# Two-layer decoder trunk on one core: VectorE's work around the MLP in another order

## The chip, the core and the metric

One core of a Trainium2 chip runs the whole program. The time is device microseconds (us) of one execution, the median of several runs. The engines are called as in the profile: PE is TensorE's matmul (PEld its weight loads), DVE is VectorE, ACT ScalarE, POOL GpSimd and SP the engine that issues the DMAs.

## What is computed

A trunk of two layers over 512 rows of 1024 columns in float32. Layer 0 mixes by a differential and a dilated attention, layer 1 by a sparse one. What the change touches is the rest of a layer, which is the same in both:

```python
h = h + rms(y, g_mix_post[i])
hn = rms(h, g_mlp_pre[i])
y = jnp.square(jax.nn.relu(hn @ w_mlp_in[i])) @ w_mlp_out[i]
h = h + rms(y, g_mlp_post[i])
gate = jax.nn.sigmoid(h @ w_ple_gate[i])
h = h + gate * (p[i] @ w_ple_proj[i])
```

`w_mlp_in` is 1024 x 4096, `w_mlp_out` 4096 x 1024, `w_ple_gate` 1024 x 1024. The result is the whole h after layer 1.

## The kernel before, in words

**Precision.** Every float32 factor is split into a high part (a cast on ACT) and a low part (the difference, on DVE or POOL). A product is three matmuls: high by high, high by low and low by high (`mm3`).

**Weights.** `Stream` (lines 123 to 166) brings all weights in one fixed sequence of units of 128x1024. SP loads a unit into one of four `raw` buffers; ACT casts it into one of four `wh` buffers (L138), and DVE subtracts into `wl` (L142), or POOL does so in two halves where the unit is marked "p". `ws.next()` takes the next unit, `ws.free(n)` gives n back; only then does `pump` issue the copies and splits of the units four places further on. So the place of `ws.free` in the program is the place of those splits in DVE's order.

**Order.** PE runs in the order of the program. Of the other engines each works through a queue that was fixed when the program was built: among the instructions that were reckoned ready, the one that stands earliest in the program goes first, so an instruction can stand in a queue ahead of others that the program has before it. On the chip a queue is worked off strictly in its order.

**First matrix (the z stage).** `layer_tail` ends the mixer's output projection row tile by row tile (four tiles of 128 rows): `post_norm` adds the normed result to h, `pre_transpose` scales it by the gain, PE transposes it, ACT and DVE split it into `hz` (L259, L260), and `pre_stats` takes the sum of squares; the inverse roots are computed on POOL (L220). The matmuls of the first four of 32 weight units are cut in halves of 256 columns, so that they begin before tiles 2 and 3 are there. `z_evac` takes each block out of PSUM (DVE L857 into a tile `t` of two buffers, then a square on ACT, L858). The splits of the units 1 and 3 are on POOL (`Z_ENG`).

**Sums of weights.** The second matrix is multiplied in the manner of Strassen and Winograd (seven products of half size instead of eight). `block_sums` (line 882) makes the sums of the weight blocks for it during the z stage: for each of 16 pairs of units four DMA loads `b`, four DVE subtractions (L891) and four DMA stores into `tsum`. Its tiles share the tags `ah` and `al` of five buffers each with the tiles `hg` and `junk` of the norms, and with the parts of the second matrix. It stands in the loop from unit 4 on, a pair in every second turn, and the last two pairs behind the loop.

**Second matrix (the y stage).** For each of 16 pairs, DVE makes sums of activation blocks (`sm`, L952 to L954; the tile has the tag `t`, which `z_evac` uses too), ACT and DVE split them (`split`, L930, L931), and PE adds the products 5, 7, 1 and 6 up in PSUM. A second pass makes the products 2, 3 and 4. In its last turn the results are put together on DVE (L1014, L1015, L1017), `post_norm` runs for all four row tiles, and then `ws.free(3)` follows (line 1019).

**Gate.** The gate's projection goes over the row tiles 0, 2, 1, 3; a tile is transposed (L253) in the middle of the one before it. It needs the gate's weight units 0 to 3. Unit 0 is split before the second pass ends, since four `wl` buffers are there and the last turn holds three; units 1 to 3 come with that `ws.free(3)`.

Of the kernel before, what the change touches and what calls it, by code (L numbers as in the profile page):

```python
# [18 lines left out]
P = 128  # L19
# [27 lines left out]


FILL_ENG = "vppvvvvpppppp"
Z_ENG = "vpvp" + "v" * (KF - 4)  # L50
G_ENG = "vvvvvvvv"
ENG_B = ("act", "pool", "act")
ENG_C = ("pool", "vec", "act")
# [4 lines left out]
def trunk_kernel(ctx, tc, A, out):  # L58
# [56 lines left out]
    def keep(n):  # L115
        st_at["keep"] += n
        assert st_at["keep"] <= 320
        return st[:, st_at["keep"] - n : st_at["keep"]]
# [194 lines left out]
            hrow[2 * q + 1] = t[:, 1, :]  # L313


    def post_norm(mp, r, ps2, gpost, ssy):
        yg = mp.tile([P, D], F32, tag="yg", bufs=2, name="yg")
        for n in range(2):
            junk = mp.tile([P, 512], F32, tag="t", bufs=2, name="junk")
            act.activation(junk, ps2[n], AF.Square, scale=1.0 / 32, accum_out=ssy[:, 2 * r + n : 2 * r + n + 1])  # L320
            vec.tensor_tensor(yg[:, n * 512 : (n + 1) * 512], ps2[n], gpost[:, n * 512 : (n + 1) * 512], op=ALU.mult)
        v = stat(1)
        vec.tensor_scalar(v, ssy[:, 2 * r : 2 * r + 1], ssy[:, 2 * r + 1 : 2 * r + 2], EPS, op0=ALU.add, op1=ALU.add)  # L323
        rs = stat(1)
        rsqrt(rs, v, 1)
        for n in range(2):
            hs = hrow[r][:, n * 512 : (n + 1) * 512]
            vec.scalar_tensor_tensor(hs, yg[:, n * 512 : (n + 1) * 512], rs, hs, op0=ALU.mult, op1=ALU.add)  # L328


    def pre_stats(mp, r, rstd):
# [491 lines left out]
    def layer_tail(i, p0, og, oT, hts, last, begin=None):  # L823
        gi = 4 * i
        with tc.tile_pool(name=f"tail{i}", bufs=1) as mp:
# [56 lines left out]
            def block_sums(j):  # L882

                b = [[mp.tile([P, 512], F32, tag=("ah", "al")[q], bufs=5, name="b") for n in range(2)] for q in range(2)]
                c = [slice(0, 512), slice(512, 1024)]
                for q in range(2):
                    for n in range(2):
                        sync.dma_start(b[q][n], A[f"w_mo{i}"][2 * j + q][:, c[n]])
                (b11, b12), (b21, b22) = b
                for d, x, y in ((b11, b12, b11), (b12, b22, b12), (b22, b22, b11), (b21, b22, b21)):  # L890
                    vec.tensor_tensor(d, x, y, op=ALU.subtract)  # L891
                for q in range(2):
                    for n in range(2):
                        sync.dma_start(tsum[i, j, q][:, c[n]], b[q][n])

            for fb in range(NB, KF):
                if fb % 2 == 0:
                    block_sums(fb // 2 - 2)
                h, l = ws.next()
                ps = bank("A", "z")  # L900
                z_part(ps, h, l, 0, 512)
                ws.free()
                z_evac(fb, ps)
            for j in range(KF // 2 - 2, KF // 2):
                block_sums(j)

            pls = [slot(4 + q, f"ple{q}").rearrange("p (r d) -> p r d", d=D) for q in range(2)]
# [25 lines left out]
            def banks(ps):  # L933
                return {p: [bank("AB"[r], f"y{p}{r}") for r in range(2)] for p in ps}
# [13 lines left out]

            for j in range(NP):
                x1, x2 = x[j]  # L950
                sm = mp.tile([P, S], F32, tag="t", bufs=2, name="sm")
                vec.tensor_tensor(sm[:, L], x1[:, R], x2[:, R], op=ALU.add)  # L952
                vec.tensor_tensor(sm[:, R], x1[:, L], x1[:, R], op=ALU.subtract)
                vec.tensor_tensor(x1[:, R], sm[:, L], x1[:, L], op=ALU.subtract)  # L954
                a, a1 = part_tiles(), part_tiles()
                split(a, slice(0, S), sm)
                split(a1, slice(0, S), x1)
                w = ws.next()
                ops = [(5, a, 0, w, 0), (7, a, 1, w, 1)]
                if j < NP - 2:  # L960
                    for r in (1, 0):
                        one(j, r, ops)
                    ws.free()
                w = ws.next()
                ops1 = [(1, a1, 0, w, 0), (6, a1, 1, w, 1)]
                if j < NP - 2:
                    for r in (1, 0):
                        one(j, r, ops1)
                    ws.free()
                else:  # L970
                    held.append((j, ops + ops1))
# [11 lines left out]
            ws.free(4)  # L983

            acc = banks((2, 3, 4))
            for j in range(0, NP, 2):
                ac, a4 = [], part_tiles(j == 0)
                for q in range(2):
                    x1, x2 = x[j + q]
                    vec.tensor_tensor(x1[:, R], x2[:, L], x1[:, R], op=ALU.subtract)  # L990
                    if q == 1:
                        split(a4, R, x1[:, R])
                    else:
                        split(a4, L, x1[:, R])
                    ac.append(part_tiles(j + q == 0))
                    split(ac[q], slice(0, S), x2)
                ops = []
                w0, w4, w1 = ws.next(), ws.next(), ws.next()
                for q, w in ((0, w0), (1, w1)):
                    ops.append([(2, ac[q], 0, w, 0), (3, a4, q, w, 1)])  # L1000
                ops4 = [[(4, ac[q], 1, w4, q)] for q in range(2)]
                if j == NP - 2:
                    new_big()
                    xg = make_xt([0, 1], [2, 3], KD, f"hg{i}")
                    ssy = keep(8)
                    for r in range(2):
                        d11, d12, d21, c22 = dt[r]
                        for q in range(2):
                            one(j + q, r, ops[q])
                        if r == 1:  # L1010
                            pre_transpose(mp, 0, None, xg)
                        for q in range(2):
                            one(j + q, r, ops4[q])
                        vec.tensor_tensor(d11, acc[2][r], d11, op=ALU.add)  # L1014
                        vec.tensor_tensor(d12, acc[3][r], d12, op=ALU.add)  # L1015
                        post_norm(mp, r, (d11, d12), gpost, ssy)
                        vec.tensor_tensor(d21, d21, acc[4][r], op=ALU.subtract)  # L1017
                        post_norm(mp, r + 2, (d21, c22), gpost, ssy)
                    ws.free(3)
                    continue  # L1020
                for r in range(2) if j == 0 else (None,):
                    rs = range(2) if r is None else (r,)
                    for q, o in ((0, ops[0]), (0, ops4[0]), (1, ops4[1]), (1, ops[1])):
                        for rr in rs:
                            one(j + q, rr, o)
                ws.free(3)
# [33 lines left out]
            for r in (2, 1, 3):  # L1060
                next(g0), next(g0)
                pre_transpose(mp, r, None, xg)
                next(g0), next(g0)
            drain(g0)
            drain(proj(xg, 512, [2] * 4, range(NR), gate1, halves=last))
# [336 lines left out]
```

## Time and profile before

| | |
|---|---|
| median of 3 runs | 1348.42 us (1345.66 to 1348.67) |
| the profiled execution | 1345.57 us, of which the span of the trace is 1343.8 us |
| PE busy | 1295.6 us (96% of the span) |
| DVE busy | 961.1 us (72%) |
| ACT busy | 656.5 us (49%) |
| POOL busy | 167.0 us (12%) |
| moved by DMA | 227.73 MB, 169 GB/s over the span |
| mean granted clock of PE | 0.987 of full speed |

The page gives busy time for each engine, a strip of 40 slices, and the chain of work that ended last; of that chain PE has 77%, DVE 13%. PE is nearly always busy, so what can be gained lies where it waits, and where it runs at a lower clock behind a wait. In the trace layer 0's z stage is at 276 to 458 us, its y stage to 617, its gate to about 680; layer 1's begin at 940, 1128 and 1283.

### The profile page before, as it was taken

The numbers are of one execution on the slowest core, as the hardware profiler recorded it, in microseconds if no ns is written. First come the engines' busy times: TensorE is split into PE (matmuls) and PEld (weight loads), VectorE is DVE, ScalarE is ACT, GpSimd is POOL, SyncE is SP. The second block draws the span as 40 slices with busy tenths as digits, with TensorE's granted clock in tenths as the row PEclk, the third lists the DMA queues.
The fourth block names the chain that finished last, engine by engine and source line by source line (L and its number), as shares of the span: only waits on it lengthen the run. The fifth ranks groups of instructions, "written<-read, shape, count | busy, mean of one in ns | idle before, by whom it ended". The sixth has DMA issues, their size and how long they took to land.

```text
span 1343.8 us, 18709 instructions
## 1 busy us (share of the span) xinstructions
PE 1295.6 (96%) x6617; PEld 1088.2 (81%) x6617; DVE 961.1 (72%) x1761; ACT 656.5 (49%) x1229; POOL 167.0 (12%) x161
## 2 busy tenths in 40 slices
PE   9999989999999899997998999999899998999978
PEld 7888878888888788886897679998888887888867
DVE  6678676476555699768568999966755567987674
ACT  4245476343222465564446668844322225656542
POOL 4212101030000000000013844311200000000000
PEclk9999999999999999998999999999999999999989
DMA  8312242369989655563243240011888896566621
GB/s 294 103 63 71 64 126 82 123 215 313 297 302 313 219 190 196 194 192 106 79 151 126 90 123 33 2 63 63 264 295 293 290 321 212 190 199 194 199 82 48
DMA packets 91534, 227.73 MB, mean 169 GB/s; under 512 B 10288, under 2 KB 11440, under 8 KB 91440
## 3 DMA queue, kind: packets, MB, share of 16 engines
q1 hardware_dynamic: 91440, 226.54, 50.8%
q8 instruction: 52, 0.85, 0.3%
q14 instruction: 42, 0.34, 0.1%
HBM read 184.55 MB, written 41.94 MB: 169 GB/s over the span
## 4 chain that ended last, share of the span: by engine, by line
PE 77%; DVE 13%; DMA 4%; issue 2%; ACT 2%; POOL 1%; SPq 1%; DVEq 0%; ACTq 0%; POOLq 0%
PE y L212 22%; PE z L212 21%; PE pj L212 21%; PE pv L212 3%; PE sc L212 3%; DMA b<-in_w_mo_dram 3%; DVE wl L142 2%; DVE work L1233 2%; PE trp L372 2%; DVE m L1232 2%; PE ak L212 1%; DVE b L891 1%; PE tr L253 1%; PE ple L212 1%; DVE h L328 1%
## 5 line engine op out<-in xcount | busy, mean ns | idle before, releaser
L142 DVE TENSOR_TENSOR wl<-raw,wh 128x1024 fp32r<-128x1024 f32 (+2 forms) x242 | 297.8, 1235 | 69.3 <-ACT wh L138 66.3
L138 ACT CAST wh<-raw 128x1024 fp32r<-128x1024 f32 (+3 forms) x254 | 261.8, 1034 | 172.3 <-PE pj L212 45.5
L212 PE MATMUL y<-wh,ah 128*128 128x512 f32 x432 | 169.6, 393 | 6.5 <-ACT ah L930 6.5
L891 DVE TENSOR_TENSOR b<-b 128x512 f32<-128x512 f32 x128 | 88.0, 691 | 121.4 <-DMA b<-in_w_mo_dram 113.0
L212 PE MATMUL y<-wh,al 128*128 128x512 f32 x432 | 169.7, 393 | 0.5 <-DVE al L931 0.5
L212 PE MATMUL y<-wl,ah 128*128 128x512 f32 x432 | 169.3, 392 | 0.0
L212 PE MATMUL pj<-wh,big 128*128 128x512 f32 (+1 forms) x444 | 151.3, 390 | 3.0 <-DVE big L260 3.0
L220 POOL TENSOR_TENSOR st<-st,mhalf 128x1 f32<-128x1 f32 (+1 forms) x41 | 29.9, 728 | 862.6 <-DVE st L323 745.2
L212 PE MATMUL z<-hz1L,wh 128*128 128x512 f32 (+1 forms) x288 | 106.1, 368 | 3.1 <-DVE hz1L L260 3.1
L212 PE MATMUL z<-hz0L,wh 128*128 128x512 f32 (+1 forms) x288 | 106.1, 368 | 2.1 <-DVE hz0L L260 2.1
L212 PE MATMUL z<-hz1H,wl 128*128 128x512 f32 (+1 forms) x288 | 106.1, 368 | 1.0 <-DVE wl L142 1.0
L212 PE MATMUL z<-hz0H,wl 128*128 128x512 f32 (+1 forms) x288 | 106.0, 368 | 0.6 <-DVE wl L142 0.6
L212 PE MATMUL z<-hz1H,wh 128*128 128x512 f32 (+1 forms) x288 | 106.2, 369 | 0.2 <-ACT hz1H L259 0.2
L212 PE MATMUL z<-hz0H,wh 128*128 128x512 f32 (+1 forms) x288 | 106.1, 368 | 0.2 <-ACT hz0H L259 0.2
L212 PEld LDWEIGHTS y<-wh,ah 128*128 128x128 f32 x432 | 81.9, 190 | 24.2 <-ACT ah L930 7.3
L212 PEld LDWEIGHTS pj<-wh,big 128*128 128x128 f32 x444 | 83.6, 190 | 21.3 <-DVE big L260 3.9
L212 PEld LDWEIGHTS y<-wh,al 128*128 128x128 f32 x432 | 81.9, 190 | 18.5 <-DVE al L931 1.3
L212 PEld LDWEIGHTS y<-wl,ah 128*128 128x128 f32 x432 | 81.8, 189 | 16.9
L858 ACT ACTIVATE a<-t 128x512 f32<-128x512 f32 x40 | 25.3, 632 | 125.5 <-DVE t L857 125.5
L212 PEld LDWEIGHTS z<-hz1L,wh 128*128 128x128 f32 x288 | 55.1, 191 | 11.9 <-DVE hz1L L260 3.3
L212 PEld LDWEIGHTS z<-hz0L,wh 128*128 128x128 f32 x288 | 55.0, 191 | 11.0 <-DVE hz0L L260 2.3
L212 PEld LDWEIGHTS z<-hz1H,wl 128*128 128x128 f32 x288 | 55.0, 191 | 10.3 <-DVE wl L142 1.6
(620 smaller groups left out, 2777.4 us busy)
## 6 DMA issues: line engine op xcount, KB each, us to landing
raw<-in_w_mi_dram SPq DMA_DIRECT2D x64, 512.0 KB, 5.1
b<-in_w_mo_dram SPq DMA_DIRECT2D x128, 256.0 KB, 5.3
tsum_dram<-b SPq DMA_DIRECT2D x128, 256.0 KB, 3.4
raw<-tsum_dram SPq DMA_DIRECT2D x32, 512.0 KB, 3.2
raw<-tsum_dram SPq DMA_DIRECT2D x64, 256.0 KB, 3.1
raw<-in_w_mo_dram SPq DMA_DIRECT2D x32, 512.0 KB, 3.7
raw<-in_w_ab_dram SPq DMA_DIRECT2D x20, 512.0 KB, 5.1
raw<-in_w_mo_dram SPq DMA_DIRECT2D x32, 256.0 KB, 2.6
```

The costliest lines, as they stand in the source:

```text
L138: act.copy(h[:, :n], raw[:, :n])
L142: (pool if e == "p" else vec).tensor_tensor(l[:, c], raw[:, c], f32(h[:, c]), op=ALU.subtract)
L212: pe.matmul(ps, a, b, start=first, stop=last, skip_group_check=True)
L220: pool.tensor_tensor(dst, src, mhalf[:, :n], op=ALU.pow)
L253: pe.transpose(ps[:, i * P : (i + 1) * P], src(k), ident)
L328: vec.scalar_tensor_tensor(hs, yg[:, n * 512 : (n + 1) * 512], rs, hs, op0=ALU.mult, op1=ALU.add)
L372: pe.transpose(ps[:, i * P : (i + 1) * P], pt[:, OFF[qt] + kt * P : OFF[qt] + (kt + 1) * P], ident)
L858: act.activation(at[-1][:, fb % 4, :], t, AF.Square)
L891: vec.tensor_tensor(d, x, y, op=ALU.subtract)
L1232: vec.max(m8, w)
L1233: vec.match_replace(w, m8, w, MARK)
```

## The change

`post_norm` takes its second half ready-made if it is given one (`done`), and its square is a function of its own. The splits of the first four units of `w_mlp_in` all go to DVE. `block_sums` begins at unit 6 instead of 4, and three pairs instead of two stand behind the loop. `sm` has a tag of its own with two buffers. In the second pass the square and the gain of the quarter that is already final (`c22`) are taken in turn j = 2. In the last turn, `post_norm` of tile 0 stands ahead of tile 0's product 4; `ws.free(3)` follows the last product; behind it come the norm of tile 2 (`low(0)`), the sums of the other half and the norm of tile 1; the norm of tile 3 (`low(1)`) stands in the gate, after the transposes of tile 2.

```diff
@@ -47,7 +47,8 @@
 
 
 FILL_ENG = "vppvvvvpppppp"
-Z_ENG = "vpvp" + "v" * (KF - 4)
+Z_ENG = "v" * KF
+SUMS = 6
 G_ENG = "vvvvvvvv"
 ENG_B = ("act", "pool", "act")
 ENG_C = ("pool", "vec", "act")
@@ -313,19 +314,24 @@
             hrow[2 * q + 1] = t[:, 1, :]
 
 
-    def post_norm(mp, r, ps2, gpost, ssy):
+
+    def post_norm(mp, r, ps2, gpost, ssy, done=None):
         yg = mp.tile([P, D], F32, tag="yg", bufs=2, name="yg")
-        for n in range(2):
-            junk = mp.tile([P, 512], F32, tag="t", bufs=2, name="junk")
-            act.activation(junk, ps2[n], AF.Square, scale=1.0 / 32, accum_out=ssy[:, 2 * r + n : 2 * r + n + 1])
-            vec.tensor_tensor(yg[:, n * 512 : (n + 1) * 512], ps2[n], gpost[:, n * 512 : (n + 1) * 512], op=ALU.mult)
+        half = [yg[:, :512], yg[:, 512:] if done is None else done]
+        for n in range(len(ps2)):
+            square(mp, r, n, ps2[n], ssy)
+            vec.tensor_tensor(half[n], ps2[n], gpost[:, n * 512 : (n + 1) * 512], op=ALU.mult)
         v = stat(1)
         vec.tensor_scalar(v, ssy[:, 2 * r : 2 * r + 1], ssy[:, 2 * r + 1 : 2 * r + 2], EPS, op0=ALU.add, op1=ALU.add)
         rs = stat(1)
         rsqrt(rs, v, 1)
         for n in range(2):
             hs = hrow[r][:, n * 512 : (n + 1) * 512]
-            vec.scalar_tensor_tensor(hs, yg[:, n * 512 : (n + 1) * 512], rs, hs, op0=ALU.mult, op1=ALU.add)
+            vec.scalar_tensor_tensor(hs, half[n], rs, hs, op0=ALU.mult, op1=ALU.add)
+
+    def square(mp, r, n, src, ssy):
+        junk = mp.tile([P, 512], F32, tag="t", bufs=2, name="junk")
+        act.activation(junk, src, AF.Square, scale=1.0 / 32, accum_out=ssy[:, 2 * r + n : 2 * r + n + 1])
 
 
     def pre_stats(mp, r, rstd):
@@ -894,14 +900,14 @@
                         sync.dma_start(tsum[i, j, q][:, c[n]], b[q][n])
 
             for fb in range(NB, KF):
-                if fb % 2 == 0:
-                    block_sums(fb // 2 - 2)
+                if fb >= SUMS and fb % 2 == 0:
+                    block_sums((fb - SUMS) // 2)
                 h, l = ws.next()
                 ps = bank("A", "z")
                 z_part(ps, h, l, 0, 512)
                 ws.free()
                 z_evac(fb, ps)
-            for j in range(KF // 2 - 2, KF // 2):
+            for j in range((KF - SUMS) // 2, KF // 2):
                 block_sums(j)
 
             pls = [slot(4 + q, f"ple{q}").rearrange("p (r d) -> p r d", d=D) for q in range(2)]
@@ -948,7 +954,7 @@
 
             for j in range(NP):
                 x1, x2 = x[j]
-                sm = mp.tile([P, S], F32, tag="t", bufs=2, name="sm")
+                sm = mp.tile([P, S], F32, tag="sm", bufs=2, name="sm")
                 vec.tensor_tensor(sm[:, L], x1[:, R], x2[:, R], op=ALU.add)
                 vec.tensor_tensor(sm[:, R], x1[:, L], x1[:, R], op=ALU.subtract)
                 vec.tensor_tensor(x1[:, R], sm[:, L], x1[:, L], op=ALU.subtract)
@@ -983,6 +989,20 @@
             ws.free(4)
 
             acc = banks((2, 3, 4))
+            ssy = keep(8)
+
+            def top(r):
+                d11, d12, d21, c22 = dt[r]
+                vec.tensor_tensor(d11, acc[2][r], d11, op=ALU.add)
+                vec.tensor_tensor(d12, acc[3][r], d12, op=ALU.add)
+                post_norm(mp, r, (d11, d12), gpost, ssy)
+
+            def low(r):
+                d11, d12, d21, c22 = dt[r]
+                if r == 0:
+                    vec.tensor_tensor(d21, d21, acc[4][r], op=ALU.subtract)
+                post_norm(mp, r + 2, (d21,), gpost, ssy, c22)
+
             for j in range(0, NP, 2):
                 ac, a4 = [], part_tiles(j == 0)
                 for q in range(2):
@@ -1002,22 +1022,28 @@
                 if j == NP - 2:
                     new_big()
                     xg = make_xt([0, 1], [2, 3], KD, f"hg{i}")
-                    ssy = keep(8)
                     for r in range(2):
                         d11, d12, d21, c22 = dt[r]
                         for q in range(2):
                             one(j + q, r, ops[q])
                         if r == 1:
                             pre_transpose(mp, 0, None, xg)
+                        else:
+                            top(0)
                         for q in range(2):
                             one(j + q, r, ops4[q])
-                        vec.tensor_tensor(d11, acc[2][r], d11, op=ALU.add)
-                        vec.tensor_tensor(d12, acc[3][r], d12, op=ALU.add)
-                        post_norm(mp, r, (d11, d12), gpost, ssy)
-                        vec.tensor_tensor(d21, d21, acc[4][r], op=ALU.subtract)
-                        post_norm(mp, r + 2, (d21, c22), gpost, ssy)
                     ws.free(3)
+                    low(0)
+                    vec.tensor_tensor(dt[1][0], acc[2][1], dt[1][0], op=ALU.add)
+                    vec.tensor_tensor(dt[1][1], acc[3][1], dt[1][1], op=ALU.add)
+                    vec.tensor_tensor(dt[1][2], dt[1][2], acc[4][1], op=ALU.subtract)
+                    post_norm(mp, 1, dt[1][:2], gpost, ssy)
                     continue
+                if j == 2:
+
+                    for r in range(2):
+                        square(mp, 2 + r, 1, dt[r][3], ssy)
+                        vec.tensor_tensor(dt[r][3], dt[r][3], gpost[:, S:], op=ALU.mult)
                 for r in range(2) if j == 0 else (None,):
                     rs = range(2) if r is None else (r,)
                     for q, o in ((0, ops[0]), (0, ops4[0]), (1, ops4[1]), (1, ops[1])):
@@ -1060,6 +1086,8 @@
             for r in (2, 1, 3):
                 next(g0), next(g0)
                 pre_transpose(mp, r, None, xg)
+                if r == 2:
+                    low(1)
                 next(g0), next(g0)
             drain(g0)
             drain(proj(xg, 512, [2] * 4, range(NR), gate1, halves=last))
```

## Rows read from the trace of the kernel before

**Rows 1.** Waits of PE: engine line waited for: us in total, times, longest us.

```profile
PE pj L212 <- DVE wl L142: 11.2, 2, 5.6
PE y L212 <- ACT ah L930: 6.5, 2, 3.2
PE z L212 <- DVE hz1L L260: 3.1, 1, 3.1
PE pj L212 <- DVE big L260: 3.0, 2, 1.5
PE z L212 <- DVE hz0L L260: 2.1, 1, 2.1
...
PE z L212 <- DVE wl L142: 1.6, 3, 0.7
```

**Rows 2.** Windows: from:to, length, busy of PE, PEld, DVE, ACT, POOL, clock, DMA, GB/s.

```profile
293.00:297.00 4.00, 4.00 (x23) 4.00 (x24) 0.34 (x1) 0.00 (x0) 0.00 (x0) 0.62 0.98 313
...
462.00:467.00 5.00, 4.78 (x13) 3.50 (x14) 4.59 (x11) 1.62 (x3) 0.00 (x0) 0.66 0.72 247
467.00:608.00 141.00, 141.00 (x623) 116.72 (x622) 118.61 (x173) 84.19 (x114) 0.00 (x0) 1.00 0.59 190
...
626.00:631.00 5.00, 4.48 (x15) 3.83 (x16) 4.56 (x6) 0.85 (x2) 0.88 (x1) 0.55 0.40 127
```

**Rows 3.** Windows of layer 1, the same columns.

```profile
958.00:962.00 4.00, 3.82 (x19) 3.82 (x20) 1.39 (x3) 0.00 (x0) 0.00 (x0) 0.57 0.90 276
962.00:1107.00 145.00, 145.00 (x680) 121.74 (x680) 83.87 (x111) 41.48 (x52) 0.00 (x0) 1.00 0.89 297
```

**Rows 4.** Timeline of PE at layer 0's gate: start us, us, operation [idle before <-releaser].

```profile
617.34 0.39 PE L212 MATMUL pj<-wh,hg0H 128*128 128x512 f32 x1
...
626.52 0.80 PE L212 MATMUL pj<-wl,hg0H 128*128 128x512 f32 x1 [5.63 <-DVE wl L142]
```

**Rows 5.** Timeline of DVE in the same stretch.

```profile
610.72 0.68 DVE L1014 TENSOR_TENSOR d<-y,d 128x512 f32<-128x512 f32 x1
...
625.25 1.22 DVE L142 TENSOR_TENSOR wl<-raw,wh 128x1024 fp32r<-128x1024 f32 x1
```

**Rows 6.** Groups of DVE, 608 to 631 us: busy us, mean ns of one, idle before.

```profile
L142 DVE TENSOR_TENSOR wl<-raw,wh 128x1024 fp32r<-128x1024 f32 x5 | 6.0, 1221 | 2.4 <-ACT wh L138 2.4
L328 DVE SCALAR_TENSOR_TENSOR h<-yg,st,h 128x512 f32<-128x512 f32 x8 | 5.7, 749 | 0.7 <-POOL st L220 0.4
```

**Rows 7.** Timeline of DVE and POOL at the start of layer 0's MLP.

```profile
274.43 2.33 DVE L142 TENSOR_TENSOR wl<-raw,wh 128x1024 fp32r<-128x1024 f32 x1
...
292.06 1.28 DVE L260 TENSOR_TENSOR hz0L<-tr,hz0H 128x512 fp32r<-128x512 f32 x2
...
274.39 7.46 POOL L142 TENSOR_TENSOR wl<-raw,wh 128x512 fp32r<-128x512 f32 x4 [1.32 <-ACT wh L138]
```

**Rows 8.** Timeline of PE, the same start.

```profile
290.34 0.38 PE L212 MATMUL z<-hz0H,wh 128*128 128x256 f32 x1 [0.24 <-ACT hz0H L259]
292.80 0.58 PE L212 MATMUL z<-hz0L,wh 128*128 128x256 f32 x1 [2.08 <-DVE hz0L L260]
```

**Rows 9.** Chain that ended last, start of layer 1's MLP: start us, us, what.

```profile
946.98 0.45 PE tr L253 x4
...
948.30 6.99 DMA b<-in_w_mo_dram
```

**Rows 10.** Timeline of DVE and PE where layer 0's second matrix begins.

```profile
453.23 0.69 DVE L857 SCALAR_TENSOR_TENSOR t<-z,rb 128x512 f32<-128x512 f32 x1 [3.31 <-PE z L212]
...
459.27 0.41 DVE L952 TENSOR_TENSOR sm<-big 128x256 f32<-128x256 f32 x1
...
461.87 0.50 PE L212 MATMUL y<-wh,ah 128*128 128x512 f32 x1 [3.24 <-ACT ah L930]
```

**Rows 11.** Timeline near the end of the first matrix: DVE of layer 0, PE of layer 1.

```profile
438.31 1.22 DVE L142 TENSOR_TENSOR wl<-raw,wh 128x1024 fp32r<-128x1024 f32 x1
...
1108.59 0.50 PE L212 MATMUL z<-hz1H,wl 128*128 128x512 f32 x1 [0.33 <-DVE wl L142]
```

## The prediction

> **What bounds the kernel now.** I read the waits of PE first, since PE is the engine with nearly all of the time. They show one pattern: PE waits long at three places of the MLP, once per layer each [rows 1], and the releaser is DVE or, behind it, ACT. Then I read the granted clock in windows round those places: behind the long waits PE runs for some microseconds near the lower of its two levels (1.2 of 2.4 GHz; 0.55 to 0.66 as a mean of the window) [rows 2, 3]. So a place costs its waits and the slow stretch behind them, length times (1 - clock). Last I read DVE's timeline to see what stood ahead of the releaser.
>
> **Gate (C).** PE has finished the second matrix and starts the gate at 617.34 [rows 4]. It waits 1.51 us for the split transposes (3.0 for both layers, two waits) and 5.63 us for the split of unit 1 [rows 1, 4]. That split begins at 625.25, although DVE has been at the norms since 610.72 without a pause [rows 5]: six sums and eight gain products of 0.68 each like the first, and eight updates of h of 0.75, lie ahead of it or around it [rows 5, 6]. The slow stretch costs 5 x (1 - 0.55) = 2.3 us [rows 2]. Sum 9.4 us per layer.
>
> **Second matrix (B).** PE waits 3.24 us at 461.87 for the first split activations: DVE begins `sm` only at 459.27 [rows 10], behind the last z block, because both take turns in the two buffers of `t`. The slow stretch costs 5 x (1 - 0.66) = 1.7 us [rows 2], and 0.2 us follows for the low part. Sum 5.1 us; the two waits of [rows 1] are alike (6.5 together, longest 3.2), so 5.1 for layer 1.
>
> **First matrix (A).** In layer 0 PE waits 0.6 us for unit 0's split, 0.24 for ACT and 2.08 for DVE's `hz0L` [rows 1, 8]; that instruction begins at 292.06 [rows 7], behind weight sums that waited for their loads. The slow stretch costs 4 x (1 - 0.62) = 1.5 [rows 2]. Sum 4.4 us. In layer 1 the wait is 3.1 [rows 1] and the slow stretch 4 x (1 - 0.57) = 1.7 [rows 3]: with 0.9 for the small ones, 5.7 us.
>
> All three together: 2 x 9.4 + 2 x 5.1 + 4.4 + 5.7 = 39.1 us, the most that the change can win there. For scale: 0.3% of the time, about what a measurement of this kernel can tell from no change, is 4 us.
>
> **The gate after the change.** Counted by starts, a 512-wide operation of DVE takes 0.6 us, an update of h 0.67, a split 1.14, each some 0.08 under its duration, since the next one begins before it ends [rows 5, 6]. From 610.72 DVE's order becomes: two sums 1.2, two gain products 1.2, a small one 0.15, 0.85 until POOL's root is there (a ready sum of tile 2, 0.6, fits in it), tile 0's h 1.35, split of unit 1 1.14, two transposed halves 1.2, tile 2's one gain product 0.75 with its small one (the other half was done in turn 2), the splits of units 2 and 3 2.3 (covering the next root), tile 2's h 1.35. That is 11.5, so tile 2 is ready at 622.2, its first half at 621.5. PE gets to its transposes 12 matmuls after 617.34; at 141 / 623 = 0.226 us each [rows 2] that is 620.05: a wait of 1.5. Behind it stand, on DVE, the sums of tile 1 (1.8), its gain products (1.35) and then tile 2's transposed half (0.6): 625.95, where PE comes at about 625.8. So 1.7 us remain, if nothing comes between. The high end is 5.5: tile 1's h (1.35) ahead of the transposed half, and a slow stretch of 2.3. I take 2.6, near the low end, since the wait of 1.5 per layer of [rows 1] is of the same size and the slow stretch stands behind the 5.6. Later tiles have 6 us between transposes for some 5 us of DVE: hidden. The two squares and two products of turn 2 lie in a pass in which DVE is busy 118.6 of 141 us [rows 2]: hidden, and if not, under 3 us per layer. Gain 6.8 per layer, 13.6.
>
> **The second matrix after.** With its own buffers `sm` of pairs 0 and 1 needs only the first four blocks, and the parts need `ah` and `al`, free once the last weight sums are stored, over 10 us ahead of the end of z. DVE stands idle before the last z blocks (3.31 us ahead of the last but one [rows 10]), so parts and low parts are there when PE comes; weight units are, as before, four ahead. I leave 0.3 us. Gain 4.8 per layer, 9.6.
>
> **The first matrix after.** POOL's four pieces run from 274.39 for 7.46 us, and DVE's split next to them takes 2.33 instead of 1.22 [rows 6, 7]. On DVE alone four splits are done at 274.43 + 4 x 1.14 = 279.0, where POOL's last ended at 281.85: DVE gets two splits more (2.3) but none of four instructions is lengthened (4.4). The 0.6 for unit 0 goes. SP's queue holds the fifth to eighth weight loads, which wait for these splits, ahead of the loads `b`; those now go out up to 2.8 us earlier, but the second of them needs a buffer that PE's transposes of tile 2 release, 0.6 earlier than before. The chain shows the price: from those transposes to the landing, 948.30 + 6.99 [rows 9], which is slow because the weight loads are still under way. With them gone I estimate 4.5; then the sums are done as the transposes of tile 3 arrive, and ACT's 0.24 and a half low part, 0.6, remain. Bounds: nothing left but these 0.8, or the wait as before (2 to 3, with its slow stretch). I take 1.0. Unit 6 as the first turn I cost at nothing: all sums already run ahead of their place in the program, and two units later (11 us at 5.4) the last would still end before z does. Gain 3.4 and 4.7 so far.
>
> But z has a second limit. DMA share is 0.89 at 297 GB/s over 145 us [rows 3], and splits of units stand on DVE behind sums that wait for `b`. In layer 0 the split of unit 29 is done at 439.45 [rows 11]; PE needs it three units of 24 matmuls (16.3) before 458.6, at 442.3: 2.9 us in hand. In layer 1 PE already waits 0.33 there [rows 11]. With the loads some 2 us earlier (between 0.6 and 2.8), layer 0 keeps its 3.4, layer 1 gets only 2.0 of 4.7. Gain 5.4.
>
> The rows put the limit where the transfers are. The Trainium skill, "SBUF — State Buffer", § A bandwidth-pool intuition that's wrong, gives about 358 GB/s between HBM and a core; by that the 43 MB of [rows 3] would take an estimated 120 us, the stage would have room, and layer 1 would keep 4.7: 1314.2 in all. The rows decide: DVE does wait there.
>
> **Sum.** 13.6 + 9.6 + 5.4 = 28.6 us off the profiled execution's 1345.57: 1317.0. That execution lies 2.85 under the median of the runs (1348.42) and at their lowest (1345.66); I leave the sum as it is.
>
> **Rivals.**
> 1. The z stage gives everything back: if the loads don't move earlier in either layer, PE stands longer near unit 29 and A gains about nothing: 1345.6 - 23.2 = 1322.4. For it: DMA share and the wait of [rows 3, 11]. Against: 2.9 us in hand in layer 0. Chance 0.18. The same section of the Trainium skill has HBM as nearly always the end-to-end bottleneck; that is this rival.
> 2. The z stage has room after all, and the gate goes near its low bound (1.7): A 8.1, B 9.6, C 15.4: 1312.5. For it: less DMA in the way at the start. Against: [rows 11]. Chance 0.14.
> 3. `sm` is early but its parts are not, since `ah` and `al` are held by the last sums: B keeps its waits, 1326.6. Against: the sums end well ahead of z. Chance 0.07.
> 4. The order at the gate comes out as before, because ready instructions may overtake: C stays, 1330.6. Against: the late splits stand behind the norms in the program, and there they are in the trace. Chance 0.04.
> 5. Slower: the parts of the first pairs, now ready early in z, take two of five buffers of `ah` and `al` before the weight sums get them and hold them until y. Then one pair of sums is under way at a time. Counting a load of 7.0 [rows 9], four subtractions of 0.6 and a store, taken at half the load, 12.9 per pair and 206 for 16, against the some 165 that z has: 40 more per layer, 1345.6 + 80 - 23 = 1402. It decides as soon as a part is handed out before the last sum. Against: in the trace `b` waits for the buffers of earlier tiles in the program's order [rows 9]. Chance 0.04.
>
> The forecast has 0.53: 1317, on its own 1312 to 1321.
>
> **Numbers.** Cases 0.53, 0.18, 0.14, 0.07 and 0.04 lie below 1341, so faster has 0.94 after a little is kept for errors of the count; slower 0.04, same 0.02. The range goes from 1307, where all 39.1 are won, to 1328, just over rival 3; only rivals 4 and 5 lie outside.
>
> **What would show it.** Right: PE's wait for `wl` at the gate gone and one of 1 to 2.5 us at the transposes of tile 2; no wait of PE at the first `y` and a clock of 1.00 there; the wait for `hz0L` under 1 us; POOL without splits there; waits of PE for `wl` near the end of layer 1's z. Wrong: a new wait of over 3 us at any of these, or weight sums that end behind z.

## The result, and the profile after

The changed kernel takes 1316.96 us (median of 4 runs, 1314.9 to 1319.21) beside 1348.32 us before (median of 4): a ratio of 0.9772 with a 95% interval of 0.9752 to 0.9792. The predicted 1317.0 is within 0.1 us of that. The parts of the sum are not so close, and the experiments are about them. The profiled execution took 1319.21 us with a span of 1317.4, the longest of the four; line numbers have moved on (the matmuls are L213 now, the weight sums L897).

The waits of PE (engine, line, waited for: us in total, times, longest), with the MLP's entries:

```profile
PE tr L254 <- issue: 3.7, 2, 1.9
...
PE tr L254 <- DVE st L343: 1.7, 2, 0.9
...
PE z L213 <- DVE hz0L L261: 0.3, 1, 0.3
PE z L213 <- DVE hz1L L261: 0.3, 1, 0.3
```

The first four entries of [rows 1] are gone or small. New are two: 1.9 us per layer at the transposes of tile 2 in the gate, and 0.9 per layer at those of tile 2 in z.

For the rest I mark three stages in PE's timeline, the same in all kernels: z from its first matmul to the start of its last, y from there to the gate's first matmul, and the gate from there to the transposes of tile 1.

| us | z, layer 0 | z, layer 1 | y, layer 0 | y, layer 1 | gate, layer 0 | gate, layer 1 |
|---|---|---|---|---|---|---|
| before | 182.47 | 184.21 | 159.10 | 159.01 | 18.69 | 18.45 |
| changed | 179.82 | 179.45 | 153.44 | 153.45 | 13.13 | 13.15 |
| gain | 2.65 | 4.76 | 5.66 | 5.56 | 5.56 | 5.30 |
| predicted | 3.4 | 2.0 | 4.8 | 4.8 | 6.8 | 6.8 |

The gains add up to 29.5 us. Where the code is the same, the profiled execution was longer, by 1.5 us ahead of the first z and by 1.6 between the gate of layer 0 and the z of layer 1, which leaves the 26.4 between the two spans (1343.8 and 1317.4). The medians are 31.4 apart; the predicted sum of 28.6 lies between.

**Gate.** PE's timeline (start, us, operation [idle before <- releaser]):

```profile
610.57 0.39 PE L213 MATMUL pj<-wh,hg0H 128*128 128x512 f32 x1
...
615.52 1.32 PE L254 MATMUL tr<-ident,h 128*128 128x128 f32 x8 [1.89 <-issue]
...
623.70 1.03 PE L254 MATMUL tr<-ident,h 128*128 128x128 f32 x8
```

DVE's timeline next to it:

```profile
603.95 0.68 DVE L996 TENSOR_TENSOR d<-y,d 128x512 f32<-128x512 f32 x1
...
611.53 2.35 DVE L143 TENSOR_TENSOR wl<-raw,wh 128x1024 fp32r<-128x1024 f32 x2
613.80 0.21 DVE L325 TENSOR_SCALAR st<-st 128x1 f32<-128x1 f32 x1
613.92 0.68 DVE L1037 TENSOR_TENSOR d<-y,d 128x512 f32<-128x512 f32 x1
614.67 0.75 DVE L330 SCALAR_TENSOR_TENSOR h<-yg,st,h 128x512 f32<-128x512 f32 x1
615.34 0.74 DVE L330 SCALAR_TENSOR_TENSOR h<-d,st,h 128x512 f32<-128x512 f32 x1
```

The profile puts the 1.89 us down to "issue", that is, to nothing it shows; but PE goes on 0.1 us after DVE has written the first half of tile 2's h (614.67 + 0.75 = 615.42). By starts the chain from 603.95 is done at 616.00, after 12.05 us where I had counted 11.5: the small instruction of tile 2 (`st`) stands behind the splits of units 2 and 3 and not ahead of them, so they no longer cover POOL's root, and a sum of tile 1 stands in between.

Windows of the changed kernel (from:to, length, busy of PE, PEld, DVE, ACT, POOL, clock, DMA, GB/s): the two gates behind that wait, the start of z behind its waits, the two starts of y, and z in both layers.

```profile
616.00:621.00 5.00, 5.00 (x19) 3.92 (x18) 4.94 (x10) 2.40 (x6) 0.55 (x1) 0.66 0.24 92
1268.00:1273.00 5.00, 5.00 (x18) 4.00 (x19) 4.93 (x10) 2.35 (x6) 0.55 (x1) 0.66 0.22 88
...
292.00:297.00 5.00, 4.64 (x37) 4.45 (x38) 2.08 (x4) 1.74 (x3) 0.00 (x0) 1.00 0.70 244
...
457.40:462.40 5.00, 5.00 (x24) 4.15 (x23) 4.31 (x6) 3.60 (x5) 0.00 (x0) 1.00 0.89 271
1109.10:1114.10 5.00, 5.00 (x23) 4.13 (x22) 3.51 (x5) 3.15 (x4) 0.00 (x0) 1.00 1.02 379
...
297.00:437.00 140.00, 140.00 (x650) 117.31 (x649) 85.42 (x117) 41.82 (x55) 0.00 (x0) 1.00 0.89 297
949.00:1089.00 140.00, 140.00 (x651) 117.32 (x650) 86.68 (x118) 42.52 (x55) 0.00 (x0) 1.00 0.89 304
```

At the gates the granted clock is 0.66 as a mean of the 5 us: 5 x (1 - 0.66) = 1.7 us lost per layer, which the prediction had left out of its sum. At y PE runs at full clock and has no wait.

**Start of z.** PE's timeline in layer 0:

```profile
284.52 0.63 PE L254 MATMUL tr<-ident,hg 128*128 128x128 f32 x4 [0.86 <-DVE st L343]
...
292.01 0.38 PE L213 MATMUL z<-hz0H,wh 128*128 128x256 f32 x1 [0.24 <-ACT hz0H L260]
292.74 0.39 PE L213 MATMUL z<-hz0L,wh 128*128 128x256 f32 x1 [0.34 <-DVE hz0L L261]
```

and DVE's:

```profile
275.96 4.63 DVE L143 TENSOR_TENSOR wl<-raw,wh 128x1024 fp32r<-128x1024 f32 x4
...
283.69 0.69 DVE L353 TENSOR_TENSOR hg<-h,gpre 128x512 f32<-128x512 f32 x1
```

Of the waits of [rows 8] ACT's 0.24 stays and DVE's 2.08 is down to 0.34, with the clock at 1.00 behind them (window from 292). In the new order of DVE's queue the second gain product of tile 2 stands behind the four splits in one row and the norm of tile 3. It begins at 283.69, and PE waits 0.86 for it, which I had not seen. (The profile names `st`, the small instruction behind the product, which the transposes do not read.)

### The profile page after: what moved, and what is told of

Its sections match the earlier page's. It is cut to its first block, busy times and chain, and to the rows that moved or that the text cites. A ratio compares the mean times of both kernels' runs of the same rounds, so it can differ in the third digit from the quotient of the medians.

```text
span 1317.4 us, 18700 instructions
## 1 busy us (share of the span) xinstructions
PE 1290.8 (98%) x6617; PEld 1085.0 (82%) x6617; DVE 959.6 (73%) x1765; ACT 655.5 (50%) x1229; POOL 152.2 (12%) x153
## 4 chain that ended last, share of the span: by engine, by line
PE 87%; DVE 8%; ACT 2%; issue 2%; POOL 1%; DMA 1%; SPq 0%; DVEq 0%; ACTq 0%; POOLq 0%
PE z L213 26%; PE y L213 23%; PE pj L213 23%; PE sc L213 4%; PE pv L213 3%; DVE work L1261 2%; PE trp L378 2%; DVE m L1260 2%; PE tr L254 1%; DVE wl L143 1%; PE ak L213 1%; PE ple L213 1%; PE trq L398 1%; PE pva L213 1%; DMA xraw<-in_xT_dram 1%
## 5 line engine op out<-in xcount | busy, mean ns | idle before, releaser
L143 DVE TENSOR_TENSOR wl<-raw,wh 128x1024 fp32r<-128x1024 f32 (+3 forms) x246 | 297.6, 1217 | 67.0 <-ACT wh L139 64.4
L897 DVE TENSOR_TENSOR b<-b 128x512 f32<-128x512 f32 x128 | 87.9, 690 | 115.9 <-DMA b<-in_w_mo_dram 107.4
L213 PE MATMUL y<-wh,ah 128*128 128x512 f32 x432 | 168.3, 390 | 0.0
L213 PE MATMUL y<-wh,al 128*128 128x512 f32 x432 | 168.1, 389 | 0.0
L213 PE MATMUL y<-wl,ah 128*128 128x512 f32 x432 | 168.1, 389 | 0.0
L213 PE MATMUL pj<-wh,big 128*128 128x512 f32 (+1 forms) x444 | 152.5, 394 | 0.0
L213 PE MATMUL z<-hz1H,wh 128*128 128x512 f32 (+1 forms) x288 | 105.6, 367 | 0.2 <-ACT hz1H L260 0.2
L213 PE MATMUL z<-hz0H,wh 128*128 128x512 f32 (+1 forms) x288 | 105.6, 367 | 0.2 <-ACT hz0H L260 0.2
L213 PE MATMUL z<-hz0L,wh 128*128 128x512 f32 (+1 forms) x288 | 105.4, 366 | 0.3 <-DVE hz0L L261 0.3
L213 PE MATMUL z<-hz1L,wh 128*128 128x512 f32 (+1 forms) x288 | 105.4, 366 | 0.3 <-DVE hz1L L261 0.3
L213 PE MATMUL z<-hz0H,wl 128*128 128x512 f32 (+1 forms) x288 | 105.5, 366 | 0.0
L213 PE MATMUL z<-hz1H,wl 128*128 128x512 f32 (+1 forms) x288 | 105.3, 366 | 0.0
L213 PEld LDWEIGHTS pj<-wh,big 128*128 128x128 f32 x444 | 84.5, 192 | 18.7 <-issue 0.7
L213 PEld LDWEIGHTS y<-wh,ah 128*128 128x128 f32 x432 | 81.1, 188 | 16.8
L213 PEld LDWEIGHTS y<-wh,al 128*128 128x128 f32 x432 | 81.1, 188 | 16.7
L213 PEld LDWEIGHTS y<-wl,ah 128*128 128x128 f32 x432 | 81.1, 188 | 16.7
L213 PEld LDWEIGHTS z<-hz0L,wh 128*128 128x128 f32 x288 | 54.3, 189 | 9.3 <-DVE hz0L L261 0.5
L213 PEld LDWEIGHTS z<-hz1L,wh 128*128 128x128 f32 x288 | 54.3, 189 | 9.3 <-DVE hz1L L261 0.5
L213 PEld LDWEIGHTS z<-hz1H,wh 128*128 128x128 f32 x288 | 54.3, 189 | 9.3 <-ACT hz1H L260 0.5
```

The costliest lines, as they stand in the source:

```text
L143: (pool if e == "p" else vec).tensor_tensor(l[:, c], raw[:, c], f32(h[:, c]), op=ALU.subtract)
L213: pe.matmul(ps, a, b, start=first, stop=last, skip_group_check=True)
```

## The experiments

Stages of all runs, as above, in us; the two kernels of the table before are left out.

| kernel | z0 | z1 | y0 | y1 | gate0 | gate1 | median, runs |
|---|---|---|---|---|---|---|---|
| b_zeng | 179.46 | 179.46 | 159.66 | 159.72 | 18.78 | 18.79 | 1340.85, 4 |
| b_sm | 183.37 | 184.01 | 153.44 | 153.44 | 18.28 | 18.42 | 1337.65, 4 |
| b_gate | 182.96 | 183.22 | 159.74 | 159.72 | 11.57 | 11.57 | 1333.20, 4 |
| b_sums | 182.98 | 183.71 | 159.82 | 159.07 | 18.84 | 18.77 | 1348.83, 10 |
| a_vpvp | 186.06 | 183.62 | 153.44 | 153.44 | 11.52 | 13.14 | 1328.02, 4 |
| a_sm_t | 179.46 | 179.46 | 159.66 | 159.75 | 11.52 | 11.52 | 1327.37, 4 |
| a_sums4 | 179.64 | 179.61 | 153.44 | 153.44 | 11.57 | 13.14 | 1318.02, 4 |
| x_more | 185.35 | 185.43 | 153.45 | 153.45 | 11.55 | 11.54 | 1327.84, 1 |
| after2 | 179.52 | 179.46 | 153.45 | 153.44 | 13.15 | 13.16 | 1318.88, 4 |
| v_gate | 179.47 | 179.80 | 153.47 | 153.44 | 10.90 | 10.92 | 1312.20, 4 |
| v_gate2 | 179.48 | 179.48 | 153.44 | 153.44 | 10.93 | 10.92 | 1313.83, 5 |
| v_both | 179.77 | 184.63 | 153.44 | 153.44 | 10.93 | 10.92 | 1315.64, 5 |

### Each part alone, on the kernel before

```diff
b_zeng: -Z_ENG = "vpvp" + "v" * (KF - 4)
        +Z_ENG = "v" * KF
b_sm:   -sm = mp.tile([P, S], F32, tag="t", bufs=2, name="sm")
        +sm = mp.tile([P, S], F32, tag="sm", bufs=2, name="sm")
b_sums: -if fb % 2 == 0: block_sums(fb // 2 - 2)
        +if fb >= 6 and fb % 2 == 0: block_sums((fb - 6) // 2)
b_gate: the diff's hunks from post_norm on, without sm's tag, SUMS = 4
```

> The kernel before with one part of the change: the splits of z units 1 and 3 on DVE. Theory: this alone makes all of z's gain, 2.7 us in layer 0 and 4.8 in layer 1 (the last z block ends that much sooner after the first), some 7 us in all; the wait for wl near unit 29 of layer 1 is gone, and a new wait of about 0.9 us stands at the transposes of tile 2. Rival, the prediction's second limit with SUMS = 6 as what lifted it: layer 1 gains 2 us and keeps waits for wl near unit 29.

> The kernel before with sm in buffers of its own. Theory: y, counted from the last z block to the first matmul of the gate, loses 5.6 us in each layer, 11.2 in all, and PE does not wait at the first y. Rival: part of y's gain comes from the sums moved or the weight units of z; then y loses under 4 us per layer here.

> The kernel before with the last turn of y, the norms and the turn j = 2 of the changed kernel, and nothing else of it. Theory: from the gate's first matmul to the transposes of tile 1 it takes 5.3 to 5.6 us less per layer, some 11 in all, with a wait of about 1.9 us at the transposes of tile 2 and a clock of 0.66 in the 5 us behind it. Rival, the prediction's sum: 6.8 per layer, 13.6 in all.

> The kernel before with the sums of weights begun at unit 6 instead of 4. Theory: nothing changes, within 1.5 us, since DVE's queue has the same order. Rival: the later first pair frees the end of layer 1's z; then its wait for wl near unit 29 goes and the time falls by 2 to 3 us.

Against the kernel before (1348.59 us, 13 runs) the ratios are 0.9938 (0.9917 to 0.9958) for b_zeng, 0.9915 (0.9900 to 0.9930) for b_sm, 0.9884 (0.9865 to 0.9903) for b_gate and 0.9996 (0.9984 to 1.0007) for b_sums: 7.7, 10.9, 15.4 and -0.2 us, 33.8 in all beside the 31.4 of the whole change. b_gate's profiled execution lacks both slow stretches that the changed kernel has at the gate, 3.2 us; that may be the difference.

- b_zeng makes all of z's gain. Layer 1 goes to 179.46 without the sums moved and without `sm`'s buffers, so the rival of a limit that SUMS lifted falls.
- b_sm makes all of y's gain. Its y, without the two squares and products of turn j = 2, is as long as that of the changed kernel which has them (153.44): they are hidden.
- b_sums does nothing, and DVE's queue is in the order of the kernel before. The number in the program is not the place in the queue.
- b_gate gains 7.1 and 6.9 us at the gate, over the 5.6 and 5.3 of the changed kernel: my expectation missed, and the prediction's 6.8 is near. DVE's order there is the same and so is PE's wait; the slow stretch is missing. The parts of this reordering were not tried one by one. b_gate, PE's timeline:

```profile
625.30 1.27 PE L254 MATMUL tr<-ident,h 128*128 128x128 f32 x8 [1.84 <-issue]
...
631.91 1.03 PE L254 MATMUL tr<-ident,h 128*128 128x128 f32 x8
```

and its windows behind the wait in both layers:

```profile
626.00:631.00 5.00, 5.00 (x24) 4.17 (x25) 4.94 (x10) 2.96 (x7) 0.55 (x1) 1.00 0.17 66
1285.00:1290.00 5.00, 5.00 (x25) 4.16 (x24) 4.93 (x10) 2.79 (x7) 0.55 (x1) 1.00 0.21 81
```

b_sm shows the rest of the mechanism at the start of z, where POOL still splits. Its PE timeline in layer 0 and layer 1's window behind the like wait of 4.0:

```profile
295.59 0.39 PE L212 MATMUL z<-hz0L,wh 128*128 128x256 f32 x1 [3.79 <-DVE hz0L L260]
```

```profile
956.90:961.90 5.00, 4.96 (x25) 4.96 (x26) 1.24 (x2) 0.01 (x1) 0.00 (x0) 0.55 0.92 299
```

DVE's timeline of b_sm ahead of it:

```profile
291.45 0.69 DVE L891 TENSOR_TENSOR b<-b 128x512 f32<-128x512 f32 x1 [2.01 <-DMA b<-in_w_mo_dram]
292.79 2.14 DVE L891 TENSOR_TENSOR b<-b 128x512 f32<-128x512 f32 x3 [0.65 <-DMA b<-in_w_mo_dram]
294.85 1.28 DVE L260 TENSOR_TENSOR hz0L<-tr,hz0H 128x512 fp32r<-128x512 f32 x2
```

The wait for `hz0L` is 2.08 in the kernel before, 2.50 in b_sums, 3.38 in b_gate and 3.79 in b_sm, with the same four subtractions ahead of it, whose first waits 0.79, 1.19, 1.58 and 2.01 us for its load: it hangs on when the loads `b` land, as the prediction had it.

### Each part undone, in the changed kernel

a_vpvp, a_sm_t and a_sums4 put back the old line of `Z_ENG`, the old tag of `sm` and `SUMS = 4`.

> The changed kernel with the splits of z units 1 and 3 back on POOL. Theory (z loses only its own waits and the slow stretch behind them, DMA is no second limit): z is 3 us longer in layer 0 and 4 to 5 in layer 1, no wait for wl near unit 29. Rival (SUMS and the buffers of sm made room at the end of z): z of layer 1 stays at 180 or so. The gate tells whether sm of its own brings the slow stretch behind the wait at tile 2: 13.1 us from its first matmul to the transposes of tile 1 if so, 11.6 if not.

> The changed kernel with sm back in the two buffers of t. Theory: y is 5.6 us longer per layer, 11 in all, and z stays at 179.5 to 179.8 in both layers. The gate tells whether the z part brings the slow stretch behind the wait at tile 2: 13.1 us from its first matmul to the transposes of tile 1 if so, 11.6 if not.

> The changed kernel with the sums of weights begun at unit 4 again. Theory: DVE's queue is the same, the time is that of the changed kernel within 1.5 us plus or minus the slow stretches at the gate (1.6 us each, none to two of them). Rival: the sums in their old place hold up layer 1's z: 2 to 3 us longer there.

Each undoes its own stage and no other: the ratios are 0.9841 (0.9818 to 0.9863), 0.9840 (0.9820 to 0.9859) and 0.9772 (0.9750 to 0.9794). In a_vpvp, layer 0's z is 6.2 us longer and not 3. Most of that is at its start: PE waits 3.74 us for `hz0L`, and the clock behind it is at its lower level throughout (0.50). PE's timeline shows waits near the end of z as well, 1.0 us together, at the first matmul of a block (put down to ACT) and for the split of its unit. The wait at the start, the window behind it and the two near the end:

```profile
296.40 0.58 PE L213 MATMUL z<-hz0L,wh 128*128 128x256 f32 x1 [3.74 <-DVE hz0L L261]
...
296.00:301.00 5.00, 4.60 (x21) 4.61 (x22) 1.08 (x3) 0.00 (x0) 0.00 (x0) 0.50 0.96 298
...
447.75 0.47 PE L213 MATMUL z<-hz0H,wh 128*128 128x512 f32 x1 [0.64 <-ACT ah L936]
...
448.79 0.50 PE L213 MATMUL z<-hz0H,wl 128*128 128x512 f32 x1 [0.34 <-DVE wl L143]
```

There the last weight sum ended 170.7 us after the first z matmul. In the kernel before it was 162.0 and 166.7 in the two layers, in b_zeng 163.2 and 164.4, in the changed kernel 166.5 and 162.4: it does not follow PE's waits at the start. So the second limit that the prediction spoke of exists, but in most of the profiled executions z ends before it bites.

a_vpvp and a_sums4 also have the gate with the slow stretch in layer 1 (13.14) and without it in layer 0 (11.5) in one execution. Windows of a_sums4:

```profile
615.00:620.00 5.00, 5.00 (x27) 4.01 (x25) 4.93 (x10) 3.00 (x7) 0.55 (x1) 1.00 0.27 98
1266.00:1271.00 5.00, 5.00 (x18) 4.00 (x19) 4.93 (x10) 2.35 (x7) 0.55 (x1) 0.66 0.20 75
```

### How much room the transfers of z have

```diff
                 act.activation(at[-1][:, fb % 4, :], t, AF.Square)
+                if 4 <= fb < 28:
+                    pool.dma_start(again[i, fb], at[-1][:, fb % 4, :])
```

(`again` is a tensor in DRAM that nobody reads.)

> The changed kernel with 24 more stores of 256 KiB in each z stage, one behind each block from 4 to 27, of values that nobody reads; DVE's queue keeps its order. Theory (the transfers set when the sums end): 6.3 MB more at some 300 GB/s are 21 us, so the last sum ends 182 to 188 us after the first z block instead of 161 to 167, and z is 8 to 20 us longer per layer, with waits of PE near its end. Rival (DVE's place in the queue sets it and the DMA engines have room): the last sum moves by under 5 us, z by under 1.

The truth, from one execution, lies between the two. The last sum ends 172.1 us after the first z matmul in both layers, and z is 5.5 and 6.0 us longer. Window of x_more over the like 140 us:

```profile
297.60:437.60 140.00, 138.73 (x639) 115.13 (x637) 80.61 (x110) 39.21 (x49) 11.03 (x20) 1.00 0.95 326
```

and PE's timeline, two of its waits:

```profile
439.30 0.47 PE L214 MATMUL z<-hz0H,wh 128*128 128x512 f32 x1 [2.01 <-DVE t L864]
...
452.44 0.50 PE L214 MATMUL z<-hz0H,wl 128*128 128x512 f32 x1 [0.67 <-DVE wl L144]
```

The DMA engines carry 326 instead of 297 GB/s and take up part of the 6.3 MB; the rest makes the sums late, the blocks behind them come out of PSUM late (`t`), and PE waits. POOL issues the added stores (11.03 us busy in the window), but that does not lengthen DVE's instructions: a split takes 1.215 us on average and a weight sum 0.690, beside 1.217 and 0.690 in the changed kernel. So the changed kernel has some room in z, less than 6.3 MB, and the next limit behind PE's own work is with the transfers. The Trainium skill, "SBUF — State Buffer", § A bandwidth-pool intuition that's wrong, has about 358 GB/s between HBM and a core; by that, an estimate, 140 us would hold 50.1 MB, the 41.6 of the changed kernel and the 6.3 as well. The run does not agree: 45.6 MB were moved, and PE waited.

### A shorter chain at the gate

In the last turn `ws.free(1)` comes three times: ahead of tile 2's norm, between its root and its update of h (behind the first sum of tile 1), and after it. Tile 1's norm moves behind tile 2's transposes, tile 3's behind tile 1's, and each tile's transposes come after three units of the tile before it (cut):

```diff
-                    ws.free(3)
-                    low(0)
+                    ws.free(1)
+                    def mid():
+                        vec.tensor_tensor(dt[1][0], acc[2][1], dt[1][0], op=ALU.add)
+                        ws.free(1)
+                    low(0, mid)
+                    ws.free(1)
...
-                next(g0), next(g0)
+                next(g0), next(g0), next(g0)
                 pre_transpose(mp, r, None, xg)
```

> The changed kernel with a shorter chain to tile 2: the small instruction of its norm and one sum ahead of the splits of gate units 2 and 3, its transposes after three units of tile 0 instead of two, and the norm of tile 1 behind them. Theory (DVE's chain sets the wait, and the slow stretch follows the wait): from the gate's first matmul to the transposes of tile 1 10.4 to 10.9 us, no wait over 0.6, clock 1.00; 4.5 to 5.5 us faster in all than the changed kernel. Rival: DVE is the limit of the stage, the wait moves to tile 1; then 11.6 or more remain and the gain is under 3 us.

> The changed kernel again, beside the shorter gate chain on the same chip. Theory (behind the wait of 1.9 us at tile 2 the slow stretch comes in some executions and not in others): 1315 to 1320, and from the gate's first matmul to the transposes of tile 1 either 11.5 or 13.1 us in each layer, nothing between. Rival (sm of its own together with the z part brings it always): 13.1 in both layers again.

> The kernel with the shorter gate chain again, beside the changed kernel. Theory: 10.9 us at the gate in both layers with a clock of 1.00, as there is no wait there for a slow stretch to follow; 1310 to 1314, 2 to 6 us under the changed kernel. Rival (the gain of the first comparison was a matter of the chip): within 1.5 us of the changed kernel.

v_gate: 0.9733 (0.9713 to 0.9752). In the second comparison, on one chip, the changed kernel has 0.9778 (0.9756 to 0.9800) and v_gate2 0.9739 (0.9714 to 0.9764): 1318.88 and 1313.83 us, 5.1 apart after 4.8 the first time. The intervals against the kernel before overlap by a little, but the slowest run of v_gate2 (1315.48) is below the fastest of after2 (1317.22). after2 itself came out as its rival had it, with 13.15 and 13.16 us at the gate; that the slow stretch always comes is still not so, as a_sums4, whose queues are in the same order, is without it in layer 0. Up to tile 1's transposes there are now 6 matmuls more (1.4 us), so the fair stretch is from the gate's first matmul of layer 1 to the last matmul: 50.5 us in the changed kernel, 47.3 in v_gate, 3.2 less. PE's timeline and window of v_gate:

```profile
614.38 1.04 PE L254 MATMUL tr<-ident,h 128*128 128x128 f32 x8
```

```profile
615.00:620.00 5.00, 5.00 (x25) 4.10 (x24) 4.75 (x9) 3.12 (x7) 0.77 (x1) 1.00 0.50 164
```

No wait at tile 2 and full clock, in four gates of four (v_gate and v_gate2). The rival that DVE is the limit falls: the same work in another order is enough.

### The wait of 0.86 us in z, taken away

```diff
                 if r == NR - 1:
+                    hg2.extend(gains(mp, 2, gpre))
                 post_norm(mp, r, (p0[r], ps), gpost, ssy)
```

(`gains` makes tile 2's two `hg`, which its transposes then use; the gate is v_gate's.)

> The shorter gate chain, and in addition the two gain products of tile 2 (hg) ahead of the norm of tile 3 at the end of the mixer's projection. Theory: the wait of 0.85 us at the transposes of tile 2 in z is gone and nothing takes its place, z 178.5 to 179.0 in both layers, the gate as in the run with the gate chain alone (10.9 us); 1.3 to 2 us faster than that run. Rival (tile 3 or the first sums become late instead): z stays at 179.4 or more.

0.9756 (0.9740 to 0.9772), 1315.64 us: no faster than v_gate. The wait is gone at tile 2 and stands at tile 3. DVE's timeline in layer 0:

```profile
290.93 1.42 DVE L913 TENSOR_TENSOR b<-b 128x512 f32<-128x512 f32 x2 [0.66 <-DMA b<-in_w_mo_dram]
292.27 1.28 DVE L261 TENSOR_TENSOR hz0L<-tr,hz0H 128x512 fp32r<-128x512 f32 x2
```

and PE's timeline in layer 0 and layer 1:

```profile
293.00 0.39 PE L213 MATMUL z<-hz0L,wh 128*128 128x256 f32 x1 [1.68 <-DVE hz0L L261]
...
941.71 0.38 PE L213 MATMUL z<-hz1L,wh 128*128 128x256 f32 x1 [2.57 <-DVE hz1L L261]
...
1074.37 0.47 PE L213 MATMUL z<-hz1H,wh 128*128 128x512 f32 x1 [0.87 <-DVE t L879]
...
1076.01 0.51 PE L213 MATMUL z<-hz1H,wl 128*128 128x512 f32 x1 [0.94 <-DVE wl L143]
```

PE comes to tile 3 earlier, but three sums that wait for their loads stand ahead of `hz1L` in DVE's queue, and those do not come earlier. In layer 0 PE waits 1.68 us in one place instead of 0.86 and 0.34 in two, and z is as long as before (179.77); in layer 1 the last sum ends late, 171.0 us after the first z matmul, and PE waits at the end too, with a slow stretch behind. The 0.86 us were not to be had this way.

## Why the prediction came out right

**The gate (C): right in the wait, wrong in the clock.** "PE gets to its transposes ... a wait of 1.5": it is 1.89. "I take 2.6, near the low end" left out the slow stretch because the wait of 1.51 of [rows 4] had none. Those rows could not have told: five matmuls, 1.4 us, lie between that wait and the one of 5.63. Measured against PE's own work of 9.1 us (36 matmuls at 0.226 and some 0.9 for the transposes), 2.5 us remain without it (18.69 - 11.57 = 7.1 gained, 6.8 predicted), and 4.1 with it. It came behind 6 of the 14 waits of 1.84 to 1.9 us at the gate, 5 of 6 in the changed kernel (after and after2) and a_sums4, and took 1.6 us each time. The bounds of 1.7 and 5.5 hold both. Had I allowed it half the time, C would have been 12 us.

**The second matrix (B): right, a little small.** No wait and full clock, as predicted. Of the 5.66 us gained in layer 0, 3.4 are the wait (3.63 us from the start of the last z to the first y before, 0.23 now), and 1.7 the slow stretch, as taken. The mis-sized terms are the small ones. I left 0.3 us, and nothing remained; and I took 0.2 for the low part, where PE's first matmuls lose 0.6. The kernel before, behind the matmul at 461.87 of [rows 10]:

```profile
462.20 0.40 PE L212 MATMUL y<-wl,ah 128*128 128x512 f32 x1
462.82 0.50 PE L212 MATMUL y<-wh,al 128*128 128x512 f32 x1 [0.22 <-DVE al L931]
463.16 0.52 PE L212 MATMUL y<-wh,ah 128*128 128x512 f32 x1
```

From 461.87 to 463.16 three matmuls take 1.29 us; at the pace of the rest of y (0.226 each) they take 0.68. In seven of the eight y stages of b_zeng, b_gate, b_sums and a_sm_t, which keep the wait, the whole is 6.2 to 6.4 us (159.66 to 159.82 less 153.44), and the slow stretch is longer: in b_zeng the clock from 462 to 467 us is 0.50, where [rows 2] have 0.66.

**The first matrix (A): the sum right in layer 0, a step wrong in layer 1.** Layer 0 has 2.65 of 3.4 in the profiled execution, 3.3 against b_gate, b_sums and b_sm taken together (183.1 - 179.8). The remainder of 1.0 is 1.4: 0.24 and 0.34 as counted and the 0.86 at tile 2, not foreseen, which v_both shows to stand ahead of the loads. The way to it was not the one counted. I had the second load `b` wait for a buffer until tile 2's transposes, and the loads land in 4.5 us. SP's timeline of layer 0, before and changed, with the first loads' size and median time to landing:

```profile
282.25 3.29 SPq L888 DMA_DIRECT2D b<-in_w_mo_dram  x6
b<-in_w_mo_dram SPq DMA_DIRECT2D x5, 256.0 KB, 5.8
...
281.00 5.53 SPq L894 DMA_DIRECT2D b<-in_w_mo_dram  x8
b<-in_w_mo_dram SPq DMA_DIRECT2D x4, 256.0 KB, 6.1
```

They go out 3.7 us after the first z matmul instead of 6.5, ahead of those transposes (283.06), and land no faster. Three sums instead of four also stand ahead of `hz0L` in the new queue. How much of the gain is due to the earlier loads, to the shorter splits and to this order was not separated. In layer 1, "z has a second limit ... layer 1 gets only 2.0 of 4.7" failed: it gets 4.76, and the waits of PE for `wl` near the end that were to show it are not there. I took one wait of 0.33 [rows 11] for the limit. It isn't there in b_sums, b_sm or b_gate, whose z is otherwise the old one. The last sum ends 160 to 167 us after the first z matmul in nearly all runs; the unit that PE waited for is split behind fewer sums in the new queue (61 instead of 64), and so is in hand by 6.6 us in layer 1 (1086.2 against the 1092.8 at which PE takes it up). The limit itself is real: x_more and a_vpvp reach it.

**SUMS** was costed at nothing, and is nothing (b_sums, a_sums4).

**The rivals.** 3 and 4 fell by the table (y and gate both gain); 5 too, as no sum was held up. 1 fell with z's full gain. 2, the case with room, was half right: z has it, the gate did not go to its low bound. So the errors of A and B (+2.0 and +1.6) and of C (-2.7) nearly cancelled. That 1317.0 lies within 0.1 us of the median is luck: the sum of 28.6 was taken off an execution 2.75 us below its own median (1345.57 and 1348.32), and the medians are 31.4 apart. By its terms the case was good to some 3 us.

## What to carry to other kernels

Read a wait together with the clock behind it, and price a wait near 2 us with and without the slow stretch; where an order without the wait can be had, it is worth more than its own length. A wait that stands ahead of another resource's arrival (here the loads) is worth nothing by itself; ask what PE meets next before it is removed. And where queues are ordered when the program is built, compare the queues, not the program: a moved line may move nothing, and a changed engine for two splits may reorder a whole stage.

## What was not expected of the hardware

- Behind waits of 1.84 to 1.9 us at the gate the clock falls in some executions and not in others, and within one execution in one layer and not in the other (a_sums4). What decides was not settled. In b_gate and a_sm_t, where PE also pauses for 3.2 us at the start of y, it fell in none of 4; where it doesn't pause there, in 6 of 10; the two of x_more, with short waits near the end of z, are among the four without. A wait of the same length (1.87 to 1.9 us, PE's `tr` for DVE's `lat` in layer 1's attention, whose code is the same in all kernels) stands once in each of the 14 traces, and the clock fell behind it in 4. Nor is the length all that counts: in v_both the wait of 2.57 us was followed by a clock of 1.00 (943 to 948 us), and 0.87 and 0.94 close together by 0.68 (1075 to 1080 us). The Trainium skill, "TensorE: Matmul & The Clock Gate", § What's actually happening, says that the number of matmuls at the lower level at a kernel's start differs between runs of one kernel; these rows show the like in mid-kernel, between the layers of one execution.
- The DMA engines, at a share of 0.89 and 297 to 304 GB/s through z, still took 326 GB/s when asked for more (x_more, share 0.95); in the first 5 us of layer 1's y they moved 379 GB/s.
